# A diffusion block followed by a hybrid layer on one core: one sum in the output projection's tiles, output matrices of the state space made during the feed-forward network, and other rules for which engine takes w_ada's steps

## The chip, the cores and the metric

The kernel is one program on 1 core of a Trainium2 chip. The metric is the device time of one execution in microseconds (us). Five engines work side by side, each in the order of its own instruction list: TensorE (PE in the profile, with its weight loads shown apart as PEld), VectorE (DVE), ScalarE (ACT), GpSimd (POOL), and the queues that issue transfers (SP's and ACT's).

## The reference, cut to what matters

Two blocks run one after the other on 256 tokens of width 2048, in float32. The first is a transformer block whose norms and gates are modulated by a conditioning vector `c`:

```python
mod = silu(c) @ w_ada + b_ada                      # w_ada: 2048 x 12288
sh1, sc1, gt1, sh2, sc2, gt2 = split(mod, 6)
h = rms_norm(x, g_norm1) * (1 + sc1) + sh1
a_out, b_out = differential and latent attention over h @ w_in
x = x + gt1 * (concat([a_out, b_out]) @ w_out)     # the output projection
h2 = rms_norm(x, g_norm2) * (1 + sc2) + sh2
x = x + gt2 * ((silu(h2 @ w_gate) * (h2 @ w_up)) @ w_down)
```

The second is a hybrid layer: a spatial gate, a state space branch (its output uses complex matrices C, scaled by factors that come from the step size and the eigenvalues), an attention over 256 memory tokens, three gated branches and an output projection.

## The kernel before, in words

Activations are kept transposed, 16 tiles of 128 features by 256 tokens. A float32 product is made of rounded halves: weight and activation are split into a high and a low part (`hi`, `lo`), and high times high, high times low and low times high are summed in PSUM. Weights come from memory in pieces of 128x1024 ("raw", 512 KB); ScalarE casts a piece to `hi`, VectorE subtracts to get `lo` (`prep_one`). At most three prepared pieces stand ready.

**The order of the work is planned while the program is written.** `Net` keeps a clock for every engine (`load`), where E is TensorE's time. `ws_tile` and `xs_chunk` write matmuls and call `tick` every second step; `tick` writes the events that are due (chains of small steps on the other engines) and calls `feed`. `until(done)` moves E on and ticks until something is ready. Nothing of this exists at run time: it sets the order on each engine.

**w_ada** is a matrix-vector product of 100 MB, read beside everything else of the first 700 us. Its 192 pieces come in six pairs of chunks, (2, 0), (3, 1), (4, 5), (8, 9), (6, 7), (10, 11), each pair 16 steps of two pieces. `issue_dma` orders transfers on SP's queue: a w_ada piece is issued only while four pieces of ordinary weights have come or are on their way, or where `need` asks for it, and at most four w_ada pieces wait. A step (`prep_ada`) runs either on VectorE, two multiply-adds over 128x1024 into `ada` (150 `ada<-raw,cact,ada` in the page), or on TensorE, four float32 matmuls with a 32-column stationary operand (`ada_pe`, L444). `feed` (L499 to L508) chooses: first a piece of ordinary weights is prepared; else, if both pieces are there within 2 us and VectorE's planned queue is at most `ada_limit` long, VectorE takes the step; else, if four pieces have come, TensorE does. When a pair is complete, `ada_columns` folds VectorE's sum into TensorE's row (`ada_pe` with ones), copies it, turns it by four transposes and adds the bias; then the chunk is in `mod_done`.

**The output projection** (`attention_block`, L1006 to L1035) follows the two attentions: 16 tiles with `mixA` and 16 with `mixB`, each of 8 steps. With `two=True` a step is one 512-column matmul (high weight, both halves of the activation, into two sums side by side) and one 256-column matmul (low weight), and `add_gated` adds both sums into x with two VectorE operations. With `two=False` a step is three 256-column matmuls into one sum. The second norm needs chunks (8, 9) and the FFN starts with a wait for (6, 7) (`ffn`, L1499). While the second norm is computed (`norm_acc`, `second_norm`), TensorE runs two early tiles on un-normed activations.

**The state space's output matrices** `cf` are made by `ssm_prepare` (L2029): two loads, then six GpSimd operations on 128x1024, called from `second` (L1719) right when the third norm (`norm_acc`, called from `second`) runs its reciprocal square root on VectorE. They are first used long after that.

Of the kernel before, what the change touches and what calls it, by code (L numbers as in the profile page):

```python
# [21 lines left out]
T = 256  # L22
D = 2048
# [14 lines left out]
AHEAD = (4, 4)  # L38
# [7 lines left out]
LIMIT = {'V': 6.0, 'S': 6.0, 'P': 6.0}  # L46
ADA_LIMIT = (3.0, 3.0, 4.0)
WS_TICK = (2, 8)
# [5 lines left out]
class Small:  # L54
# [7 lines left out]
    at = {}  # L62
    n = 0
# [202 lines left out]
class Net:  # L266
# [97 lines left out]

    def until(self, done):
        while not done():
            at = [q[0][0] for q in (self.events, self.hot) if q] + [q[0][2] - EARLY for q in self.came if q]
            wait = max(self.load[k] - LIMIT[k] for k in self.load)
            self.load.at["E"] = max(min(at), self.load.at["E"] + max(wait, 0.1))
            self.tick()  # L370

    def drain(self):
# [3 lines left out]
    def start_stream(self, items, ada, need):  # L376
        self.items, self.ada, self.need = items, ada, need
        self.i_item = self.i_ada = 0
        self.came = ([], [])
        self.ready = []  # L380
        self.free = [0.0] * N_RAW[0]
        self.n_raw = self.room = N_RAW[0]
        self.ada_limit = ADA_LIMIT[0]
        self.ada_open = False

# [112 lines left out]
    def feed(self):  # L498

        while True:  # L500
            if len(self.ready) < N_W - 1 and self.came[0] and self.here(self.came[0][0][2]):
                self.prep_one()
            elif not self.ada_open and len(self.came[1]) > 1 and self.here(self.came[1][1][2]) and self.load["V"] <= self.ada_limit:
                self.prep_ada(False)
            elif not self.ada_open and len(self.came[1]) >= AHEAD[1] and self.came[1][-1][2] < self.load.at["E"]:
                self.prep_ada(True)
            else:
                return  # L508
# [438 lines left out]
    def attention_block(self, X):  # L947
        nc = self.nc
        self.A1 = self.c([P, 16], s="A1")
        self.H = H = Pairs(self, "hh")  # L950
        order = [[(ch, 0) if ch[0] == "c" else (ch[0], int(ch[1])) for ch in o] for o in ORDER]
        self.until(lambda: {0, 2} <= self.mod_done)
        pre = self.first_mod(X, 0)
        self.steps(self.lambda_steps(), 2)
        part = {}
        for ch in order[0]:
            n, kind = (320, "w_ckv") if ch[0] == "ckv" else (512, "w_in")
# [6 lines left out]
            pre = None  # L964
        self.until(lambda: {1, 3} <= self.mod_done)
        pre = self.first_mod(X, 1)
# [12 lines left out]
        for ch in order[1]:  # L979
            n, kind = (320, "w_ckv") if ch[0] == "ckv" else (512, "w_in")  # L980
# [21 lines left out]
        for c in range(4):  # L1002
            self.xs_chunk("w_kv_b", 512, self.ckvT, 2, lambda ps, c=c: self.later(1, lambda: self.km_post(ps, c), True))
        self.ada_limit = ADA_LIMIT[2]

        self.start_mla()  # L1006
        self.until(lambda: {("mix", 0), ("mix", 1)} <= self.ready_set)
        X = []
        for m in range(16):
            if m % 8 == 0:  # L1010
                self.until(lambda: 4 + m // 8 in self.mod_done)
            if m % 4 == 0:
                for _ in range(2 if m == 0 else 1 if m < 12 else 0):
                    X.append(self.u(s="x"))
                    nc.sync.dma_start(X[-1], self.a["xT"][:, 4 * len(X) - 4:4 * len(X), :])
            self.add_gated(self.ws_tile("w_out", self.mixA, (8,), two=True), X, m, 2)
        self.until(lambda: {("mixB", h) for h in range(8)} <= self.ready_set and {8, 9} <= self.mod_done)
        A2 = self.A2 = self.c([P, 16], s="A2")
# [10 lines left out]
        for m in range(16):  # L1029
            if m % 4 == 0:  # L1030
                xa[1].append(self.u(F32R, "xl"))
            if m % 3 == 0:
                xa[0].append(self.u(F32R, "xh"))
            self.add_gated(self.ws_tile("w_out", self.mixB, (8,), two=True), X, m, 2, split)
        self.X = X  # L1035
# [5 lines left out]
    def add_gated(self, ps, X, m, part, then=None):  # L1041

        def add():
            x = self.kt(X, m)
            for v in (ps[:, :T], ps[:, T:]):
                self.nc.vector.scalar_tensor_tensor(x, v, self.modc(part, m), x, op0=ALU.mult, op1=ALU.add)
        self.chain(1, add, *([lambda: then(m)] if then else []), hot=(add,))

    def norm_acc(self, acc, done, rb=None):

        at = {}

        def sums():
            at["s"] = self.tok_sums(acc)

        def rms():
            at["r"] = self.rms(at["s"], 2, D)
            at["d"] = self.diag(at["r"])

        def rows():  # L1060
            at["p"] = self.spread(at["d"])

        def copy():
            to = self.t(s="rb")[:, :T] if rb is None else rb
            self.nc.scalar.copy(to, at["p"])
            done(at["r"], to)
        self.chain(1, sums, rms, rows, copy, hot=(rms, copy))
# [428 lines left out]
    def ffn(self):  # L1496
        nc = self.nc
        X, H = self.X, Pairs(self, "h2")
        self.until(lambda: {6, 7} <= self.mod_done)  # L1499
        self.until(lambda: "xa" in self.ready_set)  # L1500
        for j, x in enumerate(self.xa[0]):
            n = min(3, 16 - 3 * j)
            v = x[:, :(T + 2) * n].rearrange("p (k t) -> p k t", k=n)
            self.hilo(self.modc(3, 3 * j, n).unsqueeze(2), v[:, :, T:T + 1], v[:, :, T + 1:T + 2])
        self.second_norm(H)
        for c in range(FCH):
            if c == 1:
# [36 lines left out]
            for m in range(16):  # L1544
                if m % 8 == 0:
                    self.until(lambda: 10 + m // 8 in self.mod_done)
                if last and m == 0:
                    self.acc = self.t(s="acc")[:, :T]
                self.add_gated(self.ws_tile("w_down", hid, (6, 5), two=True), X, m, 5, split if last else None)
# [128 lines left out]
    def second(self):  # L1678
# [35 lines left out]
        def each(k):  # L1714
            if k % 2:
                H.units[k // 2] = None
                if N_EXACT + k // 2 < 8:
                    exact(N_EXACT + k // 2)
        self.steps(self.ssm_prepare(), 1)  # L1719
        rb = self.rb  # L1720

        def scaled(units, m, ps):
# [5 lines left out]
            self.chain(1, *stages, lambda: self.when(["rb"], mult, True), hot=stages, last=True)  # L1728
        self.two = True
        self.bx = self.units(2, s="bx")  # L1730
        for m in range(8):
# [5 lines left out]
        for m in range(8):  # L1737
# [10 lines left out]
            if m == SSM_AT:  # L1748
                self.until(lambda: "cf" in self.ready_set)
                self.start_ssm()  # L1750
# [277 lines left out]

    def ssm_prepare(self):  # L2029
        nc = self.nc  # L2030
        self.ssc = self.units(2, s="ssc")
        self.cf = self.units(2, s="cf")
        for n in range(2):
            nc.sync.dma_start(self.ssc[n], self.a["ssc"][:, n])
        c = [x.rearrange("p (j h) -> p j h", h=32) for x in self.ssc]
        o = [x.rearrange("p (j h) -> p j h", h=32) for x in self.cf]
        f = [self.f[:, n].unsqueeze(2).to_broadcast([P, NPAIR, 32]) for n in range(3)]
# [3 lines left out]
        for n, (c0, c1) in enumerate(((0, 1), (2, 0))):  # L2041
# [5 lines left out]
            yield  # L2047
        self.ready_set.add("cf")

    def ssm_early(self):  # L2050

        yield from self.ssm_setup()
        self.tabA = yield from self.ssm_powers(4)
        self.tabB = yield from self.ssm_powers(0)
# [207 lines left out]
```

## Time and profile before

| | us |
|---|---|
| median of 3 runs (lowest, highest) | 2247.77 (2245.05, 2254.02) |
| the profiled execution | 2242.02 |
| its span | 2240.20 |

| engine | busy us | share of the span |
|---|---|---|
| TensorE (matmuls) | 2137.4 | 95% |
| VectorE | 1715.2 | 77% |
| ScalarE | 1035.2 | 46% |
| GpSimd | 358.1 | 16% |

Engine rows give instructions or busy time over a stretch, in us from the start of the span; an "x8" is a count of instructions. In a timeline the bracket at a row's end is the idle time of that engine just before it, and what ended it. "clock" is the share of full TensorE speed that was granted: 1.00 is 2.4 GHz and 0.50 is 1.2 GHz.

### The profile page before, as it was taken

The numbers are of one execution on the slowest core, as the hardware profiler recorded it, in microseconds if no ns is written. First come the engines' busy times: TensorE is split into PE (matmuls) and PEld (weight loads), VectorE is DVE, ScalarE is ACT, GpSimd is POOL, SyncE is SP. The second block draws the span as 40 slices with busy tenths as digits, with TensorE's granted clock in tenths as the row PEclk, the third lists the DMA queues.
The fourth block names the chain that finished last, engine by engine and source line by source line (L and its number), as shares of the span: only waits on it lengthen the run. The fifth ranks groups of instructions, "written<-read, shape, count | busy, mean of one in ns | idle before, by whom it ended". The sixth has DMA issues, their size and how long they took to land.

```text
span 2240.2 us, 34880 instructions
## 1 busy us (share of the span) xinstructions
PE 2137.4 (95%) x13126; PEld 1872.4 (84%) x13126; DVE 1715.2 (77%) x2496; ACT 1035.2 (46%) x1665; POOL 358.1 (16%) x470
## 2 busy tenths in 40 slices
PE   6998899896899999999999999999999999999997
PEld 6777776675788888888888878889999999998886
DVE  7988799889795786866665687688877888866654
ACT  4454458443444444444444445444434343454442
POOL 2200315102000039995000030010000000000000
PEclk9999999998899999999999999999999999999999
DMA  9899878688695755875665557766656666655571
GB/s 378 300 362 346 313 247 283 235 289 337 235 361 158 242 180 171 260 254 187 180 227 175 156 195 255 229 232 200 203 189 214 205 193 218 202 183 178 178 265 57
DMA packets 159400, 519.29 MB, mean 232 GB/s; under 512 B 17496, under 2 KB 22232, under 8 KB 159232
## 3 DMA queue, kind: packets, MB, share of 16 engines
q1 hardware_dynamic: 150496, 499.89, 66.2%
q10 hardware_dynamic: 8736, 17.18, 2.1%
q8 instruction: 103, 1.69, 0.3%
q14 instruction: 65, 0.53, 0.1%
HBM read 499.15 MB, written 17.84 MB: 231 GB/s over the span
## 4 chain that ended last, share of the span: by engine, by line
PE 79%; DVE 9%; DMA 3%; POOL 3%; issue 2%; ACT 2%; ACTq 0%; DVEq 0%; SPq 0%; POOLq 0%
PE p L523 78%; DVE lo L211 2%; DVE ada L211 2%; POOL rt L211 1%; ACT hi L211 1%; POOL tab L211 1%; DVE s L211 1%; DMA raw<-in_w_gu 1%; POOL rot L211 1%; DMA raw<-in_w_ada 1%; PE p L444 1%; PE p L753 1%; DMA dV<-memV 0%; POOL tabt L211 0%; DVE rt L211 0%
## 5 line engine op out<-in xcount | busy, mean ns | idle before, releaser
L523 PE MATMUL p<-h,hi 128*128 128x256 f32 (+1 forms) x3904 | 1028.9, 338 | 6.9 <-ACT hi L211 6.9
L211 DVE TENSOR_TENSOR lo<-raw,hi 128x1024 fp32r<-128x1024 f32 (+2 forms) x740 | 878.2, 1203 | 203.2 <-ACT hi L211 196.3
L523 PE MATMUL p<-h,lo 128*128 128x256 f32 x2880 | 812.0, 282 | 1.3 <-DVE lo L211 1.2
L211 ACT CAST hi<-raw 128x1024 fp32r<-128x1024 f32 (+2 forms) x740 | 713.0, 995 | 174.9 <-DVE lo L211 62.1
L523 PEld LDWEIGHTS p<-h,hi 128*128 128x128 f32 x3904 | 669.0, 190 | 96.5 <-ACT hi L211 8.3
L523 PEld LDWEIGHTS p<-h,lo 128*128 128x128 f32 x2880 | 548.5, 190 | 2.8 <-DVE lo L211 2.5
L523 PE MATMUL p<-hid,hi 128*128 128x512 f32 x704 | 247.8, 397 | 0.1
L523 PE MATMUL p<-hid,lo 128*128 128x256 f32 x704 | 197.6, 281 | 0.0
L211 DVE SCALAR_TENSOR_TENSOR ada<-raw,cact,ada 128x1024 f32<-128x1024 f32 x150 | 191.2, 1319 | 0.0
L523 PE MATMUL p<-hi,hh 128*128 128x512 f32 (+1 forms) x512 | 158.6, 388 | 9.4 <-ACT hh L211 7.0
L523 PEld LDWEIGHTS p<-hid,hi 128*128 128x128 f32 x704 | 132.1, 188 | 32.4 <-DVE hid L211 0.4
L211 DVE SCALAR_TENSOR_TENSOR x<-p,mod,x 128x256 f32<-128x256 f32 x192 | 92.5, 482 | 53.2 <-PE p L523 49.7
L523 PEld LDWEIGHTS p<-hid,lo 128*128 128x128 f32 x704 | 133.0, 189 | 0.0
L523 PEld LDWEIGHTS p<-hi,hh 128*128 128x128 f32 x512 | 96.4, 191 | 31.9 <-ACT hh L211 7.5
L211 POOL TENSOR_TENSOR acc<-acc,sq 128x256 f32<-128x256 f32 (+1 forms) x42 | 48.3, 1150 | 392.1 <-ACT sq L211 387.9
L523 PE MATMUL p<-lo,hh 128*128 128x512 f32 (+1 forms) x256 | 98.7, 386 | 1.8 <-DVE lo L211 1.8
L211 ACT COPY sg<-p 128x256 f32<-128x256 f32 x84 | 29.6, 372 | 115.8 <-PE p L523 115.8
L211 DVE TENSOR_TENSOR sg<-p,sg 128x256 f32<-128x256 f32 x84 | 31.9, 418 | 63.6 <-ACT sg L211 63.6
L523 PE MATMUL p<-hi,m 128*128 128x512 f32 x256 | 78.9, 389 | 0.0
L211 ACT ACTIVATE gt<-p 128x256 f32<-128x256 f32 x32 | 12.3, 384 | 133.8 <-PE p L523 133.7
L211 POOL TENSOR_TENSOR rt<-tab,tab 128x256 f32<-128x256 f32 x64 | 74.0, 1157 | 0.0
L211 POOL TENSOR_TENSOR rot<-rot,rt 128x256 f32<-128x256 f32 x64 | 65.2, 1038 | 0.0
(329 smaller groups left out, 2886.1 us busy)
## 6 DMA issues: line engine op xcount, KB each, us to landing
raw<-in_w_ada SPq DMA_DIRECT2D x192, 512.0 KB
raw<-in_w_gu SPq DMA_DIRECT2D x176, 512.0 KB
raw<-in_w SPq DMA_DIRECT2D x96, 512.0 KB
raw<-in_w2g SPq DMA_DIRECT2D x96, 512.0 KB
raw<-in_w_out SPq DMA_DIRECT2D x64, 512.0 KB
raw<-in_w_in SPq DMA_DIRECT2D x56, 512.0 KB
raw<-in_w_down SPq DMA_DIRECT2D x64, 384.0 KB
raw<-in_wb SPq DMA_DIRECT2D x48, 512.0 KB
```

The lines of the kernel that those rows point to most:

```text
L211: return f(*args, **kw)
L444: self.nc.tensor.matmul(self.ada_row[32 * j:32 * j + 32, :], left, w, start=start, stop=last)
L523: self.nc.tensor.matmul(out, lhsT, rhs, start=start, stop=stop)
L753: self.nc.tensor.transpose(out, in_, self.flip if flip else self.ident)
```

## The change

One sum a tile: the 32 tiles of the output projection use `two=False`, and `add_gated` adds as many sums as there are. Output matrices: `ssm_prepare` becomes `ssm_output`, run inside `ssm_early` during the FFN, after `ssm_setup` and ahead of the tables; the result is written to memory and read back at the start of `second`; the wait for it goes. w_ada: from `w_kv_b`'s end to the second norm VectorE's limit is 1.5 instead of 4.0, and TensorE takes a step once two pieces have come instead of four; after that the limit is 3.0 (4.0 before) and four pieces are wanted again. In the waits for `mod_done` TensorE takes a step as soon as its two pieces have come by the plan, ahead of VectorE. The second norm's reciprocal square root stays on VectorE (`last` is True) and does not go to GpSimd.

```diff
-ADA_LIMIT = (3.0, 3.0, 4.0)
+ADA_LIMIT = (3.0, 3.0, 1.5)
@@ until
-    def until(self, done):
+    def until(self, done, ada=False):
+
+        self.idle = ada
         while not done():
...
+        self.idle = False
@@ start_stream
-        self.ada_open = False
+        self.ada_open = self.idle = False
+        self.ada_wait = AHEAD[1]
@@ feed
             if len(self.ready) < N_W - 1 and self.came[0] and self.here(self.came[0][0][2]):
                 self.prep_one()
+            elif not self.ada_open and len(self.came[1]) > 1 and self.came[1][1][2] < self.load.at["E"] and self.idle:
+                self.prep_ada(True)
             elif not self.ada_open and len(self.came[1]) > 1 and self.here(self.came[1][1][2]) and self.load["V"] <= self.ada_limit:
                 self.prep_ada(False)
-            elif not self.ada_open and len(self.came[1]) >= AHEAD[1] and self.came[1][-1][2] < self.load.at["E"]:
+            elif not self.ada_open and len(self.came[1]) >= self.ada_wait and self.came[1][self.ada_wait - 1][2] < self.load.at["E"]:
                 self.prep_ada(True)
@@ attention_block (the waits for mod_done all get the argument True)
-        self.until(lambda: {0, 2} <= self.mod_done)
+        self.until(lambda: {0, 2} <= self.mod_done, True)
...
-        self.ada_limit = ADA_LIMIT[2]
+        self.ada_limit, self.ada_wait = ADA_LIMIT[2], 2
...
-            self.add_gated(self.ws_tile("w_out", self.mixA, (8,), two=True), X, m, 2)
+            self.add_gated(self.ws_tile("w_out", self.mixA, (8,)), X, m, 2)
...
-            self.add_gated(self.ws_tile("w_out", self.mixB, (8,), two=True), X, m, 2, split)
+            self.add_gated(self.ws_tile("w_out", self.mixB, (8,)), X, m, 2, split)
@@ add_gated
-            for v in (ps[:, :T], ps[:, T:]):
+            for v in [ps[:, T * i:T * (i + 1)] for i in range(ps.shape[1] // T)]:
@@ norm_acc
-            at["r"] = self.rms(at["s"], 2, D)
+            at["r"] = self.rms(at["s"], 2, D, True)
@@ ffn
         self.second_norm(H)
+        self.ada_limit, self.ada_wait = ADA_LIMIT[0], AHEAD[1]
@@ second
-        self.steps(self.ssm_prepare(), 1)
...
+        self.cf = self.fetch(self.cfd, "cf")
         self.bx = self.units(2, s="bx")
...
-                self.until(lambda: "cf" in self.ready_set)
                 self.start_ssm()
@@ ssm_output (was ssm_prepare)
-        self.ssc = self.units(2, s="ssc")
-        self.cf = self.units(2, s="cf")
+        ssc, cf = self.units(2, s="ssc"), self.units(2, s="cf")
...
-        self.ready_set.add("cf")
+        self.cfd = self.spill(cf, "dC")
@@ ssm_early
         yield from self.ssm_setup()
+        yield from self.ssm_output()
         self.tabA = yield from self.ssm_powers(4)
```

## Rows read from the trace of the kernel before

**Rows 1.** The page: busy time of each engine, and TensorE in 40 slices.

```profile
PE 2137.4 (95%) x13126; PEld 1872.4 (84%) x13126; DVE 1715.2 (77%) x2496; ACT 1035.2 (46%) x1665; POOL 358.1 (16%) x470
...
PE   6998899896899999999999999999999999999997
```

**Rows 2.** Windows: stretch, busy PE PEld DVE ACT POOL (instructions), clock, DMA share, GB/s.

```profile
504.00:560.00 56.00, 37.89 (x223) 29.32 (x224) 55.54 (x70) 20.88 (x38) 12.59 (x14) 0.86 0.89 338
...
840.00:896.00 56.00, 55.88 (x323) 48.99 (x322) 38.35 (x43) 26.54 (x42) 55.45 (x67) 1.00 0.54 171
...
1064.00:1120.00 56.00, 56.00 (x319) 48.56 (x318) 34.36 (x56) 24.06 (x36) 0.00 (x0) 1.00 0.61 180
...
1568.00:1624.00 56.00, 56.00 (x465) 55.26 (x466) 48.31 (x74) 27.60 (x38) 0.00 (x0) 1.00 0.62 203
```

**Rows 3.** Timeline of TensorE, 420 to 610 us: its waits in this stage.

```profile
431.18 0.64 PE L523 MATMUL p<-mixA,hi 128*128 128x512 f32 x1 [4.31 <-DVE mixA L211]
...
559.75 3.12 PE L444 MATMUL p<-ada,ones 128*32 128x512 f32 x8 [18.11 <-DVE ada L211]
...
566.54 0.55 PE L523 MATMUL p<-xh,hi 128*128 128x258 f32 x1 [1.82 <-DVE xh L211]
...
607.27 0.80 PE L523 MATMUL p<-h,hi 128*128 128x512 f32 x1 [6.02 <-ACT hi L211]
```

**Rows 4.** Timeline of VectorE, 427 to 561 us: steps of w_ada, first and last.

```profile
427.33 2.48 DVE L211 SCALAR_TENSOR_TENSOR ada<-raw,cact,ada 128x1024 f32<-128x1024 f32 x2
...
558.43 2.47 DVE L211 SCALAR_TENSOR_TENSOR ada<-raw,cact,ada 128x1024 f32<-128x1024 f32 x2
```

**Rows 5.** Timelines of SP's queue and of TensorE: w_ada's transfers; one step on TensorE.

```profile
512.91 22.33 SPq L223 DMA_DIRECT2D raw<-in_w_ada  x18
...
378.43 1.06 PE L444 MATMUL p<-raw,crep 128*32 128x512 f32 x8
```

**Rows 6.** Instructions of two tiles, 340 to 640 us: w_ada's steps, and a releaser.

```profile
L444 PE MATMUL p<-raw,crep x96: 592/605/617, 340.3 to 597.3; 128*32 128x512 f32 x96
...
  DMA raw<-in_w_ada: 0.6, 3
...
L211 DVE SCALAR_TENSOR_TENSOR ada<-raw,cact,ada x66: 1269/1276/1764, 344.9 to 638.9; 128x1024 f32<-128x1024 f32 x66
```

**Rows 7.** Groups by line and shape: low parts of weight pieces, adds into x.

```profile
L211 DVE TENSOR_TENSOR lo<-raw,hi 128x1024 fp32r<-128x1024 f32 x596 | 743.3, 1261 | 185.8 <-ACT hi L211 179.8 <-POOL rt L211 4.2 <-issue 0.3
...
L211 DVE SCALAR_TENSOR_TENSOR x<-p,mod,x 128x256 f32<-128x256 f32 x192 | 92.5, 482 | 53.2 <-PE p L523 49.7
```

**Rows 8.** Timeline of VectorE, 572 to 583 us: the second norm.

```profile
572.16 0.16 DVE L211 TENSOR_SCALAR v<-p 128x2 f32<-128x2 f32 x1 [3.13 <-PE p L523]
...
575.58 0.48 DVE L211 TENSOR_SCALAR diag<-ident,rs 128x128 f32<-128x128 f32 x2 [2.85 <-POOL rs L211]
575.98 2.47 DVE L211 SCALAR_TENSOR_TENSOR ada<-raw,cact,ada 128x1024 f32<-128x1024 f32 x2
...
580.64 2.47 DVE L211 SCALAR_TENSOR_TENSOR ada<-raw,cact,ada 128x1024 f32<-128x1024 f32 x2
```

**Rows 9.** Timelines of VectorE and of GpSimd, 1327 to 1342 us: third norm, matrices.

```profile
1327.84 2.99 DVE L211 TENSOR_TENSOR lo<-raw,hi 128x1024 fp32r<-128x1024 f32 x1 [0.76 <-ACT hi L211]
...
1332.87 2.23 DVE L211 TENSOR_TENSOR rt<-rs 128x2 f32<-128x2 f32 x1
...
1329.70 2.90 POOL L211 TENSOR_TENSOR cft<-ssc,f 128x1024 f32<-128x1024 f32 x1
```

**Rows 10.** TensorE there: timeline, and a window of ten us.

```profile
1342.80 1.19 PE L523 MATMUL p<-diag,ones 128*128 128x256 f32 x2 [5.03 <-DVE diag L211]
...
1340.00:1350.00 10.00, 7.20 (x35) 6.25 (x36) 8.12 (x15) 3.10 (x6) 1.25 (x1) 0.83 0.47 157
```

**Rows 11.** Timelines of VectorE and of TensorE, 204 to 214 us: end of an early pair.

```profile
204.58 7.26 DVE L211 SCALAR_TENSOR_TENSOR ada<-raw,cact,ada 128x1024 f32<-128x1024 f32 x6
...
212.65 1.06 PE L444 MATMUL p<-ada,ones 128*32 128x512 f32 x8
```

More of the change, by code (lines that the diff above doesn't have):

```diff
@@ L964, in attention_block @@
             pre = None
-        self.until(lambda: {1, 3} <= self.mod_done)
+        self.until(lambda: {1, 3} <= self.mod_done, True)
         pre = self.first_mod(X, 1)
@@ L1010, in attention_block @@
             if m % 8 == 0:
-                self.until(lambda: 4 + m // 8 in self.mod_done)
+                self.until(lambda: 4 + m // 8 in self.mod_done, True)
             if m % 4 == 0:
@@ L1015, in attention_block @@
                     nc.sync.dma_start(X[-1], self.a["xT"][:, 4 * len(X) - 4:4 * len(X), :])
-            self.add_gated(self.ws_tile("w_out", self.mixA, (8,), two=True), X, m, 2)
-        self.until(lambda: {("mixB", h) for h in range(8)} <= self.ready_set and {8, 9} <= self.mod_done)
+            self.add_gated(self.ws_tile("w_out", self.mixA, (8,)), X, m, 2)
+        self.until(lambda: {("mixB", h) for h in range(8)} <= self.ready_set and {8, 9} <= self.mod_done, True)
         A2 = self.A2 = self.c([P, 16], s="A2")
@@ L1498, in ffn @@
         X, H = self.X, Pairs(self, "h2")
-        self.until(lambda: {6, 7} <= self.mod_done)
+        self.until(lambda: {6, 7} <= self.mod_done, True)
         self.until(lambda: "xa" in self.ready_set)
@@ L1545, in ffn @@
                 if m % 8 == 0:
-                    self.until(lambda: 10 + m // 8 in self.mod_done)
+                    self.until(lambda: 10 + m // 8 in self.mod_done, True)
                 if last and m == 0:
@@ L2026, in xa_head, with ssm_output @@
         self.attend(logits, 256 ** -0.5, pv, True)
-    def ssm_prepare(self):
+    def ssm_output(self):
         nc = self.nc
-        self.ssc = self.units(2, s="ssc")
-        self.cf = self.units(2, s="cf")
+        ssc, cf = self.units(2, s="ssc"), self.units(2, s="cf")
         for n in range(2):
-            nc.sync.dma_start(self.ssc[n], self.a["ssc"][:, n])
-        c = [x.rearrange("p (j h) -> p j h", h=32) for x in self.ssc]
-        o = [x.rearrange("p (j h) -> p j h", h=32) for x in self.cf]
+            nc.sync.dma_start(ssc[n], self.a["ssc"][:, n])
+        c = [x.rearrange("p (j h) -> p j h", h=32) for x in ssc]
+        o = [x.rearrange("p (j h) -> p j h", h=32) for x in cf]
         f = [self.f[:, n].unsqueeze(2).to_broadcast([P, NPAIR, 32]) for n in range(3)]
```

## The prediction, made before the result was known

> **What bounds the kernel now.** I read the page first. TensorE is busy for 2137 of 2240 us, and the slices show where the missing 103 us are: almost all in the first eleven slices and the last [rows 1]. Next the windows. In the FFN and the second block TensorE fills every stretch, 56.00 of 56, so no other engine's work there can shorten anything; in 504 to 560 us it has 37.89, VectorE 55.54, and the clock is at 0.86 [rows 2]. So the change can win only ahead of 610 us and where a wait stands alone. Then TensorE's own waits. Around the output projection they are 4.3 us before the tiles, 18.1 us after them and 6.0 us before the FFN proper [rows 3]. The tiles are through at 541.65 (the fold at 559.75 less its wait), and the wait ends with VectorE's last step of w_ada at 558.43, whose six last steps stand behind 541 [rows 3, 4]. VectorE, not the transfers, is late: SP issued this pair's last 18 pieces between 512.9 and 535.2, 1.24 us each [rows 5]. One more wait is at 1337.8: 5.0 us for the third norm's diagonal [rows 10].
>
> **The matrices made early.** While GpSimd runs its six large operations, VectorE's work on two numbers takes 2.23 us instead of 0.16 us, and a `lo` 2.99 us instead of 1.26 [rows 7 to 9]. Read off that timeline, the excess of six such operations is some 10.6 us, so without them the diagonal is ready near 1332, ahead of TensorE, which comes to it at 1337.8. That returns the 5.0 us and the clock: ten us at 0.83 hold 3.4 us at 1.2 GHz, which cost 1.7 [rows 10]. I take **-6.7**; it is -3 if a weight piece or the fetch is late instead, and not below -6.7. In their new place the same operations (about 13.4 us, the longest 2.90) [rows 9] meet an FFN in which GpSimd is already busy for 55.45 of 56 us in one stretch, and TensorE loses 0.12 us there [rows 2]: cost 0. SP carries two loads earlier and two fetches in their old place; ScalarE's queue gets two issues behind GpSimd's last operation, and the casts behind them could wait about one operation, 2.9 us, under three prepared pieces of some 2.8 us each (eight steps of 0.35). Transfers are busy for 0.61 of a full stretch [rows 2], so 2 MB more are hidden. If this cover went, the price is at most the 13.4 us.
>
> Both slowed VectorE operations read two inputs from SBUF [rows 9]. The Trainium skill, SBUF — State Buffer, section "Who interferes with whom", calls the port that VectorE shares with GpSimd an exclusive lock, which a VectorE operation with two SBUF inputs contends for against a GpSimd operation that reads SBUF; it speaks against the move, as the block is only carried into the FFN, where each `lo` has two such inputs. By the rule that is up to 13.4 us of blocked VectorE there; by the row, TensorE stays full.
>
> **One sum a tile.** 465 short matmuls take 56 us, 0.1204 each; 319 in pairs of long and short take 56 us, 0.351 a pair [rows 2]. Three short ones are 0.361, so 256 steps cost **+2.6** on TensorE. VectorE drops 32 adds of 0.48 us, 15.4 us [rows 7].
>
> **w_ada's steps.** One step is 1.06 us on TensorE [rows 5] and two times 1.27 on VectorE; from 340 to 640 us 96 matmul records, eight a step, are 12 steps, and 66 multiply-adds are 33 on VectorE, the first step of each pair left out [rows 6]. From 427.33 to 558.43, counted in the timeline, 23 steps are left, 17 of them on VectorE [rows 4]. How many move is not in the trace; the bounds are 5 and 17. A tile of the second half keeps VectorE 2.2 us (`lo` 1.26, one add and one scaling of 0.48) in 2.9 us, so over 32 tiles 22 us stay free, room for nine steps; the limit of 1.5 wants the queue nearly empty, so I give it five and move 12: **+12.7** on TensorE. In return go the 4.3 us wait before the tiles, where VectorE was at a step from 427.33 [rows 3, 4], and the half clock behind it, 1.4 (five pairs of 0.64 us, not 0.35): **-5.7**. The tiles then end at 541.65 + 2.6 + 12.7 - 5.7 = 551.3. Transfers keep up: 46 pieces and 32 of w_out at 1.24 us are 97 us of some 125. Behind the last step stand fold, copy, turn and bias, 559.75 to 566.54, with a fold of 3.12 us at half clock [rows 3]; at full clock I take 1.06 for it, so 4.7. TensorE resumes at 556.0 and not 566.5: **-10.5**.
>
> **Second norm.** The sums waited 3.13 us for TensorE at half clock: -2. The square root waited 2.85 us for GpSimd; twelve VectorE operations of 0.17 in its place: -1. Two steps of w_ada, 4.9 us, stand between the diagonal and the normed tiles [rows 8]; a limit of 3.0 keeps one off: -2.5 (bounds 0 and -6, the whole wait at 607 [rows 3]). Costs: the stricter limit may push one last-pair step onto the full TensorE: +1 (bounds 0 and +4). At the early pairs three steps back to back end just as TensorE comes free at 212.65 [rows 11]; on TensorE they could add up to 3.2 at each of two places, or save 1 each: 0, as the plan offers VectorE the step first when its queue is within 3.0.
>
> **Sum.** -6.7 - 10.5 - 2 - 1 - 2.5 + 1 = -21.7 (the +2.6, +12.7 and -5.7 are in the -10.5). The profiled execution took 2242.0, 1.8 more than its span and 5.8 below the median of the runs; it becomes 2220.3. Against the median, 2247.8, I forecast **2226**.
>
> **Rivals.**
> A. *TensorE becomes the bound of this stage.* All 17 steps move (+18.0), tiles end at 556.6, TensorE resumes at 561.3 (-5.2), four steps of the last pair land on it in the FFN (+4.2), the norm gains 1: -6.7 - 5.2 + 4.2 - 1 = -8.7, 2239. For it: TensorE is full in this stage apart from the waits named. Against: VectorE's limit still lets it in.
> B. *Slower: TensorE waits, in order, for pieces that have not landed.* The plan's arrival time decides when a step is written, and VectorE's lateness no longer pads it. With four pieces wanted the waits were 0.6 us in three places [rows 6]; the margin given up is two pieces, 2.5 us. With 18 steps on TensorE the gain is gone at 1.2 us a step and 11 us are lost at 1.8; at the full 2.5 it is +45, 2271. Against: with buffers free, pieces follow at 1.24 us [rows 5], so a second piece is late by that, not by 2.5. The matmuls behind each long wait take 0.64 a pair for 0.35. The Trainium skill, TensorE: Matmul & The Clock Gate, section "HAM oscillation — how this bites in real kernels", describes this, matmuls in bursts between transfers that fall back to the low clock each time; no run here shows it yet.
> C. *The steps stay on VectorE*, the plan's queue being short: then the adds alone free VectorE, 16 tiles of 0.52 = 8.3 us: -6.7 - 8.3 - 1 + 1 = -15, 2233.
>
> **How the numbers follow.** 0.5%, 11.2 us, is about what a measurement of this kernel can tell from no change: faster is under 2236.5, slower over 2259. The forecast (2212 to 2236) has 0.50, C 0.14, A 0.22, B 0.10, and 0.04 is for more than forecast. Faster: 0.50 + 0.12 of C + 0.04 + 0.04 of A, about 0.69; slower 0.10, all B; same 0.21. The range reaches down to 2210 (five steps move, 7.4 less, the norm 3.5 more, the early pairs 2, in part together) and up to 2247, A with 6 lost at the early pairs; B and the far end are left out.
>
> **What would show it.** Right: no wait of TensorE at the third norm's diagonal, VectorE's small operations there at 0.16; 512 `mixA` and `mixB` `hi` matmuls of 256 columns, 32 fewer adds; about 24 steps on TensorE from 340 to 640 and no 18 us wait; the FFN proper starting near 588. Wrong: waits of TensorE's steps on w_ada's transfers of over 1 us each (B), the tiles ending after 556 (A), or 12 VectorE steps still behind 480 us (C).

## The result, and the profile after

The changed kernel took **2215.28 us** (median of 4 runs, 2206.76 to 2216.06) and the kernel before, measured with it, 2247.53 (4 runs): ratio 0.9841 [0.9814, 0.9869]. Measured again later, on chip 1, the same program gave 0.9887 [0.9865, 0.9909], 2218.85 against 2246.05. Predicted were 2226 and "faster" (with a chance of about 0.69). The profiled executions took 2242.02 before and 2215.38 after, spans 2240.2 and 2213.7; the 26.5 us between the spans are what follows.

The page of the changed kernel, the lines that answer to [rows 1]:

```profile
span 2213.7 us, 35400 instructions
PE 2139.6 (97%) x13414; PEld 1886.2 (85%) x13414; DVE 1688.1 (76%) x2465; ACT 1035.6 (47%) x1665; POOL 358.6 (16%) x460
...
PE   6998899999999999999999999999999999999997
```

TensorE's busy time has grown by 2 us while the span lost 26: the weak slices 8, 10 and 11 (8, 6 and 8 tenths before) are at 9, that is 90% or more. TensorE's own waits, from its timeline, answer to [rows 3]:

```profile
542.14 0.39 PE L529 MATMUL p<-xh,hi 128*128 128x258 f32 x1 [4.34 <-DVE xh L211]
580.12 0.78 PE L529 MATMUL p<-h,hi 128*128 128x512 f32 x1 [3.98 <-ACT hi L211]
867.54 0.47 PE L529 MATMUL p<-hid,hi 128*128 128x512 f32 x1 [1.70 <-DVE hid L211]
870.34 0.80 PE L529 MATMUL p<-hid,hi 128*128 128x512 f32 x1 [2.21 <-DVE hid L211]
```

The tiles end at 537.8 (541.65 before), nothing is folded behind them, and TensorE resumes at 542.14 and not at 566.54. The wait of 18.1 us has become one of 4.3, the 6.0 ahead of the FFN proper one of 4.0. Two waits are new, in the middle of the FFN, and the one at the third norm's diagonal [rows 10] is gone. Cut at four marks that both kernels have (matmuls' starts in us), and at the end:

| mark | before | after | won up to here |
|---|---|---|---|
| TensorE resumes behind the tiles (`xh,hi`) | 566.54 | 542.14 | 24.4 |
| FFN proper (`h,hi` behind the wait) | 607.27 | 580.12 | 27.2 |
| last matmul of `w_down` (`hid,lo`) | 1324.37 | 1303.59 | 20.8 |
| first use of `cf` | 1454.1 | 1426.1 | 28.0 |
| end of the span | 2240.2 | 2213.7 | 26.5 |

So the output projection gave 24.4, the second norm 2.8, the FFN took 6.4 back, the third norm gave 7.2, and 1.5 went between the first use of `cf` and the end.

**Where the steps went.** Windows of the changed kernel, columns as in [rows 2]; the first lies ahead of the tiles, the second and third beside them, the last in the FFN:

```profile
365.00:431.00 66.00, 61.55 (x343) 37.76 (x340) 58.16 (x118) 49.27 (x164) 18.90 (x41) 0.97 0.85 293
431.00:485.00 54.00, 53.61 (x420) 49.09 (x419) 45.61 (x58) 20.94 (x26) 0.00 (x0) 1.00 0.93 333
485.00:545.00 60.00, 55.66 (x449) 51.57 (x448) 56.67 (x76) 30.96 (x57) 12.40 (x15) 0.98 0.96 350
...
840.00:896.00 56.00, 52.09 (x289) 45.05 (x288) 40.81 (x49) 24.03 (x38) 55.45 (x69) 0.97 0.57 182
```

The same three windows of the kernel before:

```profile
365.00:431.00 66.00, 55.78 (x284) 37.04 (x276) 59.53 (x116) 48.85 (x161) 20.40 (x39) 0.95 0.74 256
431.00:485.00 54.00, 50.96 (x279) 40.69 (x280) 41.19 (x64) 18.64 (x26) 0.00 (x0) 0.97 0.75 254
485.00:545.00 60.00, 56.64 (x331) 45.88 (x329) 59.33 (x81) 23.18 (x41) 10.11 (x13) 0.99 0.85 310
```

From 365 to 431 us TensorE stood idle for 10.2 us of 66: some 6 in waits for the attentions, and the 4.3 for `mixA` [rows 3]. In the changed kernel it works 5.8 us more there, and the transfers rise from 256 to 293 and then from 254 to 333 GB/s. I take it that a piece that is used sooner gives its buffer back sooner; no run changes the buffers alone. The instructions of two tiles, answering to [rows 6] (first line: 340 to 429.1 us, ahead of the tiles; the others 340 to 640):

```profile
L448 PE MATMUL p<-raw,crep x72: 592/617/1062, 340.7 to 428.6; 128*32 128x512 f32 x72
...
L448 PE MATMUL p<-raw,crep x128: 592/617/1062, 340.7 to 572.2; 128*32 128x512 f32 x128
...
  DMA raw<-in_w_ada: 1.0, 2
L211 DVE SCALAR_TENSOR_TENSOR ada<-raw,cact,ada x68: 1270/1278/1822, 345.3 to 631.6; 128x1024 f32<-128x1024 f32 x68
```

Eight records are a step. TensorE does 16 steps from 340 to 640 us and not 12; **nine stand ahead of the tiles where four stood, and beside the tiles it does one fewer than before** (five, six before). The pair that the FFN waits for is started on VectorE at 447.43 (483.3 before), and is folded and turned before the tiles end. VectorE's timeline at its start, and where the tiles end:

```profile
447.43 1.41 DVE L211 TENSOR_SCALAR ada<-raw,cact 128x1024 f32<-128x1024 f32 x2
...
536.06 0.23 DVE L211 TENSOR_TENSOR mod<-p,small 128x8 f32<-128x8 f32 x2
536.21 0.82 DVE L211 SCALAR_TENSOR_TENSOR xl<-x,A,xh 128x256 fp32r<-128x256 f32 x1
536.95 1.40 DVE L211 TENSOR_SCALAR ada<-raw,cact 128x1024 f32<-128x1024 f32 x2
538.27 0.47 DVE L211 SCALAR_TENSOR_TENSOR x<-p,mod,x 128x256 f32<-128x256 f32 x1
538.67 2.94 DVE L211 SCALAR_TENSOR_TENSOR ada<-raw,cact,ada 128x1024 f32<-128x1024 f32 x2
541.53 0.47 DVE L211 SCALAR_TENSOR_TENSOR xl<-x,A,xh 128x256 fp32r<-128x256 f32 x1
541.93 0.52 DVE L211 TENSOR_TENSOR xh<-mod,xh 128x3 fp32r<-128x3 f32 x6
```

At 536.06 the bias is added to the turned row, ahead of the tiles' end at 537.8. What is late next, 4.3 us, is one step of the last pair (538.67) that stands between the last tile's add and its rounded halves. The adds are 32 fewer, as [rows 7] (group by shape):

```profile
L211 DVE SCALAR_TENSOR_TENSOR x<-p,mod,x 128x256 f32<-128x256 f32 x160 | 77.2, 483 | 53.3 <-PE p L529 50.8
```

**What the FFN took back.** ScalarE's timeline at the first rotation table, and VectorE's and GpSimd's beside it:

```profile
851.67 0.37 ACT L211 COPY sg<-p 128x256 f32<-128x256 f32 x1
858.91 0.33 ACTq L223 DMA_DIRECT2D dR<-rot  x1
859.34 0.83 ACT L211 CAST hi<-raw 128x768 fp32r<-128x768 f32 x1 [7.30 <-POOL rot L211]
...
860.20 2.40 DVE L211 TENSOR_TENSOR lo<-raw,hi 128x768 fp32r<-128x768 f32 x2 [7.65 <-ACT hi L211]
...
857.46 1.43 POOL L211 TENSOR_TENSOR rot<-rot,rt 128x256 f32<-128x256 f32 x2
```

The store of a table is issued by ScalarE, in its order. GpSimd ends the table at 858.89; ScalarE has stood since 852, the cast behind the store comes 7.30 us late, VectorE's `lo` behind that, `hid` behind that, and TensorE waits twice. Before, the first store cost ScalarE 3.41 us and TensorE nothing. The FFN runs in four rounds of gate and up (`h`) and `w_down` (`hid`); the lengths from round two on, each from its first matmul to the next stretch's, place the loss, for both kernels and for three of the experiments below:

| stretch, us | before | after | matrices alone | behind the tables | stores from SP |
|---|---|---|---|---|---|
| 2nd gate and up | 122.03 | 122.03 | 124.38 | 124.37 | 122.03 |
| 2nd `w_down` | 62.50 | **68.03** | 65.18 | 62.19 | 61.01 |
| 3rd gate and up | 124.38 | 124.38 | 124.37 | **128.16** | **128.92** |
| 3rd `w_down` | 62.18 | 62.18 | 62.19 | 61.02 | 61.02 |
| 4th gate and up | 124.38 | 124.38 | 124.37 | 122.02 | 122.02 |

The changed kernel loses 5.5 us in one stretch, 3.9 in the two waits and the rest to the half clock behind them (mean granted clock 0.86 from 864 to 876 us). An undisturbed stretch takes either 122.0 and 61.0 or 124.4 and 62.2: TensorE has two paces (last section), and a difference that only they make isn't the change's.

### The profile page after: what moved, and what is told of

It reads as the page before. It is cut to its first block, busy times and chain, and to the rows that moved or that the text cites. A ratio compares the mean times of both kernels' runs of the same rounds, so it can differ in the third digit from the quotient of the medians.

```text
span 2213.7 us, 35400 instructions
## 1 busy us (share of the span) xinstructions
PE 2139.6 (97%) x13414; PEld 1886.2 (85%) x13414; DVE 1688.1 (76%) x2465; ACT 1035.6 (47%) x1665; POOL 358.6 (16%) x460
## 4 chain that ended last, share of the span: by engine, by line
PE 84%; DVE 6%; POOL 3%; issue 2%; ACT 2%; DMA 2%; ACTq 0%; SPq 0%; DVEq 0%; POOLq 0%
PE p L529 82%; DVE lo L211 2%; DVE ada L211 2%; POOL tab L211 1%; ACT hi L211 1%; PE p L448 1%; PE p L759 1%; DMA raw<-in_w_ada 1%; POOL rt L211 1%; POOL tabt L211 1%; DMA raw<-in_w_in 0%; POOL cf L211 0%; DVE s L211 0%; DVE lg L211 0%; DMA raw<-in_wk 0%
## 5 line engine op out<-in xcount | busy, mean ns | idle before, releaser
L211 DVE SCALAR_TENSOR_TENSOR ada<-raw,cact,ada 128x1024 f32<-128x1024 f32 x142 | 182.7, 1332 | 0.0
L211 DVE SCALAR_TENSOR_TENSOR x<-p,mod,x 128x256 f32<-128x256 f32 x160 | 77.2, 483 | 53.3 <-PE p L529 50.8
L211 ACT ACTIVATE gt<-p 128x256 f32<-128x256 f32 x32 | 12.3, 383 | 134.6 <-PE p L529 134.6
L211 POOL TENSOR_TENSOR rot<-rot,rt 128x256 f32<-128x256 f32 x64 | 74.6, 1184 | 0.0
L211 POOL TENSOR_TENSOR rt<-tab,tab 128x256 f32<-128x256 f32 x64 | 66.3, 1036 | 0.0
```

The lines of the kernel that those rows point to most:

```text
L211: return f(*args, **kw)
```

## The experiments

No kernel leaves out a part of the computation. In the expectations theory 3 is that the FFN's loss is ScalarE standing in order behind GpSimd, and theory 4 that the steps put into TensorE's waits ahead of the tiles are what sped up the stage; of the others each expectation says what it holds. "FFN proper" is the matmul's start, 607.27 before and 580.12 after. That mark is good to some microseconds: in four profiles whose instruction lists are the same up to there it lies between 579.7 and 580.7, in a fifth (the stores from GpSimd, below) at 587.1, of which that trace was 3.1 us late already at 340 us. The median is good to some 0.2%. The first four experiments ran on chip 5, the others on chip 1.

**One sum a tile alone.**

```diff
-            self.add_gated(self.ws_tile("w_out", self.mixA, (8,), two=True), X, m, 2)
+            self.add_gated(self.ws_tile("w_out", self.mixA, (8,)), X, m, 2)
```

> The kernel before with one part of the change: one sum in the 32 tiles of the output projection, one add a tile. Its program has 11 steps of w_ada on TensorE where the kernel before has 15. Theory 1 (the new rules for w_ada's steps take the wait behind the tiles): the dropped adds free VectorE of 15.4 us, of which about 8 count in the second half; the wait of 18.1 us falls to about 10, the FFN proper starts near 600; about -8 us, ratio 0.9965. Theory 2 (VectorE was the limit, and freeing it of the adds is what counts, wherever the steps run): the wait behind the tiles is under 6 us, the FFN proper starts at 580 to 588, about -20 us, ratio 0.991.

Measured: 2236.65 us against 2244.30, ratio 0.9959 [0.9945, 0.9973]; FFN proper 600.71, 6.6 earlier; the wait behind the tiles stays (timeline of TensorE):

```profile
553.83 3.12 PE L444 MATMUL p<-ada,ones 128*32 128x512 f32 x8 [16.82 <-DVE ada L211]
```

With VectorE freed the plan gives it more steps: TensorE does 8 from 340 to 640, four fewer. The adds are worth 6.6 us, near the 8.3 that rival C gave them. Theory 1 had the start of the FFN right (near 600) but not the wait, which was to fall to about 10: it is 16.8, and the tiles end earlier, at 537.0.

**The rules alone**, limit 1.5 and two pieces, back to 3.0 and four behind the second norm:

```diff
-ADA_LIMIT = (3.0, 3.0, 4.0)
+ADA_LIMIT = (3.0, 3.0, 1.5)
...
+        self.ada_limit, self.ada_wait = ADA_LIMIT[2], 2
```

> The kernel before with one part of the change: the limit of 1.5, two pieces in place of four, and both reset at the second norm. Its program has 25 steps of w_ada on TensorE where the kernel before has 15. Theory 1 (the rules take the wait): ten steps at 1.06 us go onto TensorE, the wait of 18.1 us goes, the FFN proper starts at 585 to 592, about -18 us, ratio 0.992. Theory 2 (the adds were the limit): the tiles end ten us later, near 552, a wait stays, the FFN proper starts at 597 or later, -5 us or less, ratio 0.998 or more.

Measured: 2221.82 us, 0.9902 [0.9879, 0.9925]; FFN proper 584.48, 22.8 earlier; 22 steps on TensorE from 340 to 640, nine ahead of the tiles; 4.9 us still at the third norm's diagonal. From FFN proper to the last `w_down` it takes 717.3 us, as before (717.1): without the matrices nothing is lost there. Theory 1 holds here: the rules take the wait even with two adds a tile.

**The matrices alone.** The edits of `ssm_output`, `second` and `ssm_early` on the kernel before.

> The kernel before with one part of the change: the state space's output matrices made in the FFN's second chunk and stored. The prediction's step: -6.7 us, all of it at the third norm, nothing lost in the FFN; ratio 0.9970. Theory 3 (GpSimd gets behind, ScalarE's queue stands at the store of a rotation table that GpSimd has not finished, and the casts behind it come late): about 6.7 won at the third norm, about 5.5 lost ahead of the second chunk's w_down, sum -1; ratio 0.9995.

Measured: 2242.56 us, 0.9984 [0.9969, 1.0000]: 1.7 us by the medians, between 0 and 7 by the interval, not the whole 6.7 of the prediction. The diagonal's wait is gone, but one of 2.21 is new at 900.81, and the second `w_down` is 2.7 us longer than before (65.18), with ScalarE 6.15 us at a table's store there. So the matrices take back part of their own gain even without the other edits. In the changed kernel two waits and 5.5 us stand there, but its other edits need not be the reason. With ScalarE issuing the stores and the matrices ahead of the tables there are six profiles: the four with two waits (the changed kernel twice, and below all steps on TensorE and the limit at 4.0) have 122.0 us in the second gate and up, the two with one wait (this one, and the limit of 1.5 with four pieces) 124.4. All steps on TensorE has both waits although its FFN starts later than that of the kernel before. How early TensorE comes to the stretch by its pace goes with the loss; how far ahead the FFN starts does not. The medians of the three parts give 0.41 + 0.98 + 0.16 = 1.55%, the whole 1.59%, and 1.13% when measured again.

**The matrices behind the tables.**

```diff
-        yield from self.ssm_output()
         self.tabA = yield from self.ssm_powers(4)
...
+        yield from self.ssm_output()
         self.tabA = self.tabB = None
```

> The changed kernel with the six matrix operations behind the rotation tables and not ahead of them. Theory 3 (ScalarE's queue stands at a table's store because GpSimd is 13 us behind): TensorE's two waits ahead of the second chunk's w_down, 1.7 and 2.2 us, and the half clock after them go, and nothing comes in their place: 5 to 6 us below the changed kernel, about 0.9745 of before where the changed kernel has 0.984 less 0.0025. Rival (VectorE is blocked by GpSimd wherever the operations stand): the loss moves to the new place, the time is that of the changed kernel.

(The ratio in it has a slip: 0.984 less 0.0025 is 0.9815.) Measured: 2213.05 us, 0.9853 [0.9824, 0.9882], not to be told from the changed kernel's. The tables begin 21 us earlier (800.6, not 821.6) and the waits at 867 and 870 are gone, but one of 2.24 is new at 1040.6, beside the matrices' new place; by the table 5.8 us are won in the second `w_down` and 3.8 lost in the third gate and up. The loss goes where the matrices go, as the rival said; that nothing comes in its place, as theory 3 had it, did not hold.

**The changed kernel again**, on the chip of the experiments that follow:

> The changed kernel again, beside the three that follow, so that they are compared on one chip: 0.984 of before.

Measured: 0.9887 [0.9865, 0.9909], all waits in place (4.34, 3.98, 1.68, 2.22).

**The rules only ahead of the tiles**, reset at the first tile:

```diff
+        self.ada_limit, self.ada_wait = ADA_LIMIT[2], 2
...
         self.until(lambda: {("mix", 0), ("mix", 1)} <= self.ready_set)
         X = []
+        self.ada_limit, self.ada_wait = 4.0, AHEAD[1]
```

> The kernel before with the new rules for w_ada's steps only from w_kv_b's end to the first tile of the output projection; from there on limit 4.0 and four pieces, as before. Theory 1 (the steps beside the tiles are what counts): the wait behind the tiles falls by little, under a third of the 0.98% that the rules brought alone, ratio 0.997 or more. Theory 4 (what counts are the five steps that go into TensorE's waits ahead of the tiles: their pieces give their buffers back, and the transfers run at over 330 GB/s from there in place of 255): more than two thirds, ratio 0.9935 or less.

**The rules only beside the tiles**, set there instead:

```diff
+        self.ada_limit = 4.0
...
         X = []
+        self.ada_limit, self.ada_wait = ADA_LIMIT[2], 2
```

> The kernel before with the new rules only from the first tile of the output projection to the second norm, limit 4.0 and four pieces ahead of it and behind it. Theory 1: most of the 0.98%, ratio 0.993 or less. Theory 4: the 4.3 us wait ahead of the tiles stays, transfers stay at about 255 GB/s until 430, and a wait of over 5 us stays behind the tiles; ratio 0.995 or more.

Measured: ahead 2229.35 us against 2246.05, 0.9932 [0.9911, 0.9952]; beside 2232.70, 0.9951 [0.9934, 0.9968]. TensorE's waits behind the tiles, first the one, then the other kernel:

```profile
548.46 2.26 PE L445 MATMUL p<-ada,ones 128*32 128x512 f32 x6 [13.60 <-DVE ada L211]
```

```profile
558.48 0.55 PE L524 MATMUL p<-xh,hi 128*128 128x258 f32 x1 [6.00 <-DVE xh L211]
```

FFN proper starts at 594.51 and 597.72, 12.8 and 9.6 us earlier than before; but the second trace is 2.7 us late from its first step of w_ada on (343.0, 340.3 before), ahead of every difference between the programs, so 9.6 is rather 12.3. The rules whole gave 22.8. Ahead of the tiles five more steps (nine, not four) buy some 13 us, with the tiles over at 534.9. Beside them five more steps (eleven, not six) push TensorE's work in the tiles to 552.5 and buy some 12 all the same, as the wait behind them falls. The intervals exclude both of theory 1's ratios, and theory 4's are just met (0.68 of the 0.98% is its two thirds). So the steps ahead of the tiles give between half and two thirds of what the rules bring, the steps beside them the rest.

**All steps of the stage on TensorE**, limit -1:

```diff
-ADA_LIMIT = (3.0, 3.0, 1.5)
+ADA_LIMIT = (3.0, 3.0, -1.0)
```

> The changed kernel with a limit under zero in place of 1.5: from w_kv_b's end to the second norm every step of w_ada goes to TensorE. Its program has 51 steps there where the changed one has 19. The prediction's price of 1.06 us a step and its rival A: TensorE is full beside the tiles, so some 20 to 30 of the 34 us appear, the tiles end 12 to 18 us later, and the time is 15 to 30 us above the changed kernel, ratio 0.991 to 0.997. Rival: the steps find waits of TensorE to stand in and VectorE, relieved, is never late: within 5 us of the changed kernel.

Measured: 2242.39 us, 0.9985 [0.9968, 1.0002], 23.5 above the changed kernel on the same chip. Windows of this kernel beside the tiles:

```profile
431.00:485.00 54.00, 54.00 (x398) 38.62 (x391) 23.20 (x44) 21.99 (x36) 0.00 (x0) 1.00 0.87 318
485.00:545.00 60.00, 60.00 (x480) 47.93 (x482) 31.74 (x43) 19.67 (x30) 5.34 (x7) 1.00 0.98 354
```

TensorE is full, VectorE half idle. 384 records are 48 steps in place of 16; FFN proper starts 30.2 us later, 0.94 us for each of the 32, and the tiles end 34 us later (571.9), where 12 to 18 were expected. That is rival A: real, and VectorE's share of the steps is what keeps it off.

**The tables' stores from SP's queue**, and **from GpSimd itself**:

```diff
-            self.nc.scalar.dma_start(self.rotd[j], e)
+            self.nc.sync.dma_start(self.rotd[j], e)
```

```diff
-            self.nc.scalar.dma_start(self.rotd[j], e)
+            self.nc.gpsimd.dma_start(self.rotd[j], e)
```

> The changed kernel, the 32 stores of the rotation tables issued on SP's queue and not on ScalarE's; TensorE's, VectorE's and GpSimd's instruction lists are the same. Theory 3 (what the matrices cost in the FFN is ScalarE standing in order at a store whose table GpSimd has not finished): ScalarE's 7.3 us wait for GpSimd and TensorE's waits of 1.7 and 2.2 us near 868 are gone, FFN proper to last w_down matmul takes 723 to 725 us where the changed kernel took 723.3 less 4 to 5, so about 718.5, and the span is 4 to 5 us under 2213.7, 2209; ratio 0.982 to 0.987. Rival 1 (VectorE's lo is late because GpSimd disturbs its operands): the waits near 868 stay, span 2213 to 2215. Rival 2 (the stall is carried to SP's queue, where the weight transfers stand behind the store): waits for transfers of 1 to 4 us take their place, span 2212 to 2217.

> The changed kernel, the 32 stores of the rotation tables issued by GpSimd itself, behind the operation that makes the table: nobody else's queue can stand at them. Theory 3: the waits near 868 gone as well, span near 2209, ratio 0.982 to 0.987; GpSimd pays 32 issues, which TensorE does not see. If VectorE's operand reads are what is late (rival 1), the waits near 868 stay and the span is 2213 to 2215.

From SP: the waits near 868 are gone and the second `w_down` takes 61.01 us, so theory 3 holds for the place of the loss: it was ScalarE's stand at the store. But another stretch pays. One wait is new (timeline of TensorE):

```profile
1037.97 0.80 PE L529 MATMUL p<-h,hi 128*128 128x512 f32 x1 [3.46 <-ACT hi L211]
```

A cast of ScalarE, which issues no store of a table in this kernel, stood 12.13 us there, until GpSimd's last `rt` ended at 1036.84, and the third gate and up takes 128.92. That is not rival 2, since no transfer is waited for: GpSimd itself is late, and TensorE begins this stretch 7.5 us earlier than in the changed kernel (923.07, 930.59), where the same cast came at 1041.1 and cost nothing. What the cast needs of GpSimd was not looked up. The profiled span is 7.1 shorter, 2206.6, of which 4.7 are the faster pace behind that (1.2 and 2.4 in the table's last rows, 1.2 in the 4th `w_down`). The median is 2214.53 against 2243.67, 0.9870 [0.9850, 0.9889], between the two ratios of the changed kernel: no gain is shown.

From GpSimd: **2298.70 us, 1.0242 [1.0223, 1.0260]**, which no theory expected. VectorE's and GpSimd's timelines, then the lists of waits from 930 to 1012 us (the last line is from SP's own), of this kernel:

```profile
878.47 8.38 DVE L211 TENSOR_TENSOR lo<-raw,hi 128x640 fp32r<-128x640 f32 x2
886.77 0.99 DVE L211 SCALAR_TENSOR_TENSOR x<-p,mod,x 128x256 f32<-128x256 f32 x2
...
881.72 0.58 POOL L223 DMA_DIRECT2D dR<-rot  x1 [0.30 <-POOL rot L211]
882.32 0.64 POOL L211 TENSOR_TENSOR rot<-tab,tab 128x256 f32<-128x256 f32 x1
...
886.33 0.58 POOL L223 DMA_DIRECT2D dR<-rot  x1 [0.30 <-POOL rot L211]
...
ACT hi L211 <- POOL rt L211: 54.6, 1, 54.6
...
PE p L529 <- ACT hi L211: 28.1, 1, 28.1
...
PE p L529 <- DVE lo L211: 18.9, 12, 2.7
...
SPq L223 <- POOL rt L211: 55.2, 1, 55.2
```

The two `lo` of a row have 640 and 768 columns and take 3.65 and 4.82 us here (last section). One ends in each of GpSimd's pauses at a store, every 4.61 us, and TensorE waits up to 2.7 us for it. Behind that ScalarE and SP stand 55 us for GpSimd's last table, and TensorE 28 us; the second `w_down` takes 153.7 us.

**Each rule alone in the changed kernel**: the limit at 4.0 with two pieces, and the limit of 1.5 with four.

```diff
-ADA_LIMIT = (3.0, 3.0, 1.5)
+ADA_LIMIT = (3.0, 3.0, 4.0)
```

```diff
-        self.ada_limit, self.ada_wait = ADA_LIMIT[2], 2
+        self.ada_limit, self.ada_wait = ADA_LIMIT[2], AHEAD[1]
```

> The changed kernel with VectorE's limit in this stage at 4.0 again, two pieces kept. The program has 15 steps on TensorE in place of 19. If the steps in TensorE's waits ahead of the tiles come from the two-piece rule (theory 4), about 7 stand there and the FFN proper starts within 6 us of the changed kernel's 580.1; if they come from VectorE's limit, 3 stand there as before the change and the FFN proper starts near 592 to 600. Span 2214 to 2222 or 2226 to 2234.

> The changed kernel with four pieces wanted again for a step on TensorE, the limit of 1.5 kept. The program has 15 steps on TensorE in place of 19. If the two-piece rule puts the steps ahead of the tiles (theory 4), only about 3 or 4 stand there and the FFN proper starts near 592 to 600, span 2226 to 2234; if VectorE's limit does, about 7 stand there and the span is 2214 to 2222.

Measured: 2221.70 and 2221.12 us, ratios 0.9898 [0.9879, 0.9916] and 0.9899 [0.9883, 0.9915]. The rows of w_ada's steps ahead of the tiles, of the one and of the other:

```profile
L448 PE MATMUL p<-raw,crep x48: 592/605/617, 340.9 to 420.3; 128*32 128x512 f32 x48
```

```profile
L448 PE MATMUL p<-raw,crep x48: 592/605/617, 340.9 to 435.1; 128*32 128x512 f32 x48
```

Six steps stand there in both, between the four of before and the nine of the change, and FFN proper starts at 589.53 and 594.15. My alternative, the one rule or the other, was wrong: against 600.71 with neither (one sum alone) two pieces give 11.2 us, the limit 6.6, both 20.6. The same six steps come 15 us later with four pieces, and from 365 to 431 us the transfers run at 221 GB/s there against 288: if the 4.6 us between the two starts are more than the spread of that mark, the moment counts and not only the number. By the ratios neither kernel is told from the changed one (0.9887 on this chip), so that the limit and the two pieces are both needed is not shown by the time.

## Why the prediction was right, and where its steps failed

The time fell inside the range, 11 us under the forecast, and in part by luck, because two large terms were off on opposite sides. Against the terms of the sum the stage gave 13.9 us more, the FFN took 6.4, the second norm gave 1.7 less, the third 0.5 more, and 1.5 went later: 4.8 in all. The rest is the 5.8 us by which the profiled execution before lay under its median.

- **"-10.5" for the stage: the failed step.** Measured 24.4. What failed is "I give it five and move 12": it put the moved steps beside the tiles at full price, +12.7, and the tiles' end at 551.3. The tiles ended at 537.8, and without the 12.7 the prediction's own sum gives 538.6. "About 24 steps on TensorE" were 16, one fewer than before beside the tiles. Five more went ahead of them, from 365 to 431 us, which the prediction did not price (its timelines began at 420 and 427 us). They put the tiles' start back by 3.9 us (429.14, 425.22 before), and in return TensorE's idle time between the tiles' start and end fell from 7.2 to 0.4 us. The chain "behind the last step", 4.7, was hidden, as the pair was folded inside the tiles; but the 4.3 us wait for a step of the last pair stood in its place, so this part cost the number little. With the rules beside the tiles alone TensorE's work in the tiles ended at 552.5, near 551.3, by luck: five steps moved there and not 12, the two sums and a wait of 4.2 us at the tiles' start were still in place, and the trace was 2.7 us late.
- **The matrices' new place, "cost 0".** Measured 5.5 us in one stretch of the FFN, 6.4 over the whole. The prediction named the right queue ("ScalarE's queue gets two issues behind GpSimd's last operation") but the wrong stores: not the two of the matrices but the 32 of the tables behind them, which GpSimd reaches some 21 us later (800.6 to 821.6, the kernel with the matrices behind the tables against the changed one). The stall was 7.3 us and not 2.9. Three prepared pieces did not cover it: what TensorE lacked was not a piece but `hid`, which stood behind the late `lo` on VectorE. The matrices alone lost 2.7 there, with TensorE at its slower pace.
- **The shared port, for which the prediction named the Trainium skill.** TensorE's two waits came by ScalarE's order, as the run with the stores on SP's queue shows for the stretch that lost. But GpSimd is slower beside VectorE too (its `rt` 0.90 us in the changed kernel, 0.62 in the one with GpSimd's own stores), so part of its lateness may be the port; no run separates that. The run with the stores on GpSimd shows VectorE held off for long.
- **"-6.7" at the third norm:** 7.2 between the last `w_down` and the first use of `cf`; VectorE's small operations there take 0.16 us, and the wait is gone. Right: in all nine profiles with the matrices in the FFN this stretch is 6.6 to 7.5 us shorter than in the kernel before.
- **Second norm, "-2", "-1", "-2.5":** 2.8 of 5.5. The square root stays on VectorE, but two steps of w_ada still stand between the diagonal and the normed tiles (VectorE's timeline at 550.02 and 554.68): the limit of 3.0 kept none off. The argument `True` of that square root need not be its reason: the kernel with the rules alone leaves it out, and its square root is on VectorE too (552.07 to 553.7). Up to 380 us TensorE's instruction list is the same before and after, so the steps in the waits for the early pairs change nothing and the prediction's 0 for them was exact; whether those in the later waits matter, no run shows.
- **One sum, "+2.6":** covered, the 6.6 us that it brings alone contain it.
- **Rivals.** A is real (all on TensorE, +30.2 us at the FFN's start) but did not come, as VectorE still took most of the steps. B did not come: steps on TensorE waited 1.0 us for transfers, in two places. C's condition came in part, as VectorE kept most of the steps (34 from 340 to 640 us, 33 before); but they came sooner, and the gain was not that of the adds alone. (The chances of "faster" add to 0.70, not 0.69.)

## What to carry to other kernels

Before pricing work that is moved to a full engine, look for that engine's waits ahead of the stage too: work that fits there costs little, and here it came with faster transfers. When an operation is put ahead of others on a slow producer, everything behind it comes later: check every queue that holds an instruction for that producer, above all a store that an engine with other work issues for someone else. Changing who issues such a store can be far worse than the stall: test it.

## What was not expected of the hardware

**Two paces of TensorE at a granted clock of 1.00.** Groups by shape in the changed kernel, from 800 to 840 us and from 1150 to 1230 us:

```profile
L529 PE MATMUL p<-h,hi 128*128 128x512 f32 x116 | 40.3, 391 | 0.0
```

```profile
L529 PE MATMUL p<-h,hi 128*128 128x512 f32 x228 | 80.6, 399 | 0.0
```

391 or 399 ns for the same matmul, 2% apart, with the clock column at 1.00 in both stretches. In the table a kernel changes pace only in a stretch that also holds waits (before 0.12 us [rows 2]), in either direction. What sets it stays open; it moves a span by several us with no instruction behind it.

**GpSimd against VectorE.**

Kept busy and pausing only for its own stores, GpSimd slowed VectorE's subtraction of two SBUF tiles to about a fifth of its speed: one of 640 and one of 768 columns take 8.38 us together (878.47), and 1.68 behind GpSimd's last table (1012.84). In the changed kernel, with the same table operations running, they take about 2.5. Groups by shape, first the changed kernel from 868 to 925 us, then the one with GpSimd's stores from 878 to 979 us:

```profile
L211 DVE TENSOR_TENSOR lo<-raw,hi 128x768 fp32r<-128x768 f32 x14 | 19.8, 1416 | 0.0
...
L211 POOL TENSOR_TENSOR rt<-tab,tab 128x256 f32<-128x256 f32 x20 | 18.0, 899 | 0.0
L211 DVE TENSOR_TENSOR lo<-raw,hi 128x640 fp32r<-128x640 f32 x15 | 15.9, 1060 | 0.0
```

```profile
L211 DVE TENSOR_TENSOR lo<-raw,hi 128x768 fp32r<-128x768 f32 x11 | 53.0, 4818 | 0.0
L211 DVE TENSOR_TENSOR lo<-raw,hi 128x640 fp32r<-128x640 f32 x11 | 40.1, 3649 | 0.0
...
L211 POOL TENSOR_TENSOR rt<-tab,tab 128x256 f32<-128x256 f32 x44 | 27.3, 620 | 0.0
```

In the first both engines pay (GpSimd's `rt` 0.90 us); in the second GpSimd pays nothing (0.62) and VectorE everything. The Trainium skill, SBUF — State Buffer, section "Who interferes with whom", calls the shared port an exclusive lock; the second kernel's trace agrees in that one `lo` ends in each pause. But there VectorE does not get through between the six operations of a table either, and in the first kernel, where GpSimd hardly pauses, it does. Why that is so was not tried and stays open.
